# FFN buffers at the right end of SBUF, opened before the output projection; small token block last; layer norms by half blocks; the last f's products reordered

## The chip, the core and the metric

The kernel runs on one core of a Trainium2 chip. The metric is device time of one execution in microseconds (us), as the median of several runs. The engines are named as in the profile: PE (TensorE; PEld its weight loads), DVE (VectorE), ACT (ScalarE), POOL (GpSimd) and SP (SyncE, which here issues the DMAs, all in one queue). The order of the instructions on each engine is fixed when the kernel is built; while it runs, each engine works through its own row and waits at an instruction until what it needs is there.

## The reference

One decoder layer on 2048 prompt tokens, 16 meta tokens and 32 sample tokens, in fp32: two token mixers (retention and gated delta net), an output projection, and a dense FFN, each followed by a residual and a layer norm. The change touches the last part:

```python
def layer_norm(x, g, b):
    mu = jnp.mean(x, -1, keepdims=True)
    var = jnp.mean(jnp.square(x - mu), -1, keepdims=True)
    return (x - mu) * lax.rsqrt(var + LN_EPS) * g + b

def swiglu(h, w_gate_up, w_down):          # 1024 -> 2 x 2816 -> 1024
    gu = h @ w_gate_up
    return (jax.nn.silu(gu[..., :D_FF]) * gu[..., D_FF:]) @ w_down

hp = layer_norm(ALPHA * hp + mixed, ln1_g, ln1_b)
hp = layer_norm(ALPHA * hp + swiglu(hp, w_gate_up, w_down), ln2_g, ln2_b)   # and so for the samples hs
```

The outputs are the layer's result for the 2048 prompt tokens and the 32 sample tokens, and the new mixer states.

## The kernel before

`attention()` computes the input projection and both mixers (0 to about 1350 us) and leaves the mixed activations in DRAM (`mixd`). `project()` and `ffn()` follow.

Precision: every fp32 operand of a product is split into a high and a low fp32r part (`split`, L309 the copy, mostly on ACT, and L316 the difference on DVE or POOL), and `mm3` (L366) sums three matmuls, high x high, high x low, low x high.

`project()` walks over 17 tiles of tokens: 16 of 128 prompt tokens and one of the 32 sample tokens, in the order of the FFN's blocks. For tile i it runs 48 matmuls into two PSUM banks (tile `d`), evicts them with the residual (DVE, L1175), makes the layer norm, and writes `yd` (L1177) for the FFN's residual. Two tiles later it transposes the tile (PE, `tr`, L1185; ACT copies it to `xr`, L1186). When both tiles of a pair are transposed, POOL makes four sums `T` (L1198), and seven DMAs (L1205) write the pair's parts and sums to DRAM, to `bd`. A tile's inputs are fetched one tile ahead (`mr<-mixd`, `oy<-xhat`).

`ffn()` treats the tokens in three blocks. A block takes its tokens as pairs, so that a product of a 2 x 2 split of gate and up weights with a 2 x 2 split of the activations is made with seven block products instead of eight; n is the column count of such a product. Block 0 is the small one (four prompt tiles and the sample tile, n = 272), blocks 1 and 2 have six prompt tiles each (n = 384). For each block the seven token operands (b11, t2, t1, b21, t3, t4, b22) come back from `bd` through the ring `fr` (L1370) and are split (`tokens`). Then f runs from 0 to 21, over slices of 128 of the 2816 hidden columns. For f, `weights(f)` fetches 1 MB through `fr` (L1250), POOL makes four sums `S` (L1264), and a11, a12, a22 and the sums s12, s34 are split on ACT and DVE; this happens while f - 1 is computed. `gateup` runs the seven products X, Y, Z, X2, Y2, W, Z2 (12 matmuls each), and DVE and ACT combine them (`x1`, `u2`, `u3`, `z5`) and make silu(gate) x up as `fh`, `fl`. The down products of two f, one unit per half tile of tokens (six matmuls into a PSUM bank `d`, then an addition to `y` by DVE, L1356, for the first two f L1354), are spread over the next f by `step`: one unit per step, at most twelve per pair of f. Behind the last unit of a tile stands its layer norm and the DMA of its output (L1359): bn_stats (L284), bn_aggr (L287), rsqrt by bit shift and three Newton steps on a single column (L261 to L268, ten instructions on DVE), `lnnm` (L297), ACT for scale and bias (L300), DVE for the gain (L302), POOL for the offset (L304). Only the very last tile takes the short form on DVE alone (L291, L293). A block's last down units and layer norms therefore run during the next block's f = 0 and 1, together with that block's token splits. In the last block the last two f are handled one at a time (three units per step in f = 21), and what is left is run at the end.

All of FFN's SBUF pools are opened in `ffn()`, after the projection's were closed. Where they lie on memory that the projection or the attention used, their first writers wait until the last readers of that memory are done.

## Time and profile before

| | |
|---|---|
| median of 3 runs | 3085.02 us (3084.47 to 3089.49) |
| the profiled execution | 3085.82 us, span 3084.0 us |
| mean granted PE clock | 0.972 |
| busy in the span | PE 2889.0, DVE 2189.5, ACT 1139.4, POOL 1055.6 us |

Times in a trace count from the start of its span. The span ends with the last recorded instruction or transfer; the execution's own time is 1.82 us longer. A row of a group gives the line, engine, operation, `out<-in`, shapes and count, then busy us and mean ns, then the engine's idle time just before and what ended it. A busy PE need not be at full rate: the granted clock of a stretch (1.00 is full) stands beside it in the windows. One instruction's duration includes what it waits for inside the engine.

### The profile page before, as it was taken

To read this page: it belongs to the slowest core of one execution; us is meant where nothing else is said; L and a number is where in the kernel's file an instruction comes from. 1 tells how busy PE (TensorE), PEld (TensorE's weight loads), DVE (VectorE), ACT (ScalarE), POOL (GpSimd) and SP (SyncE) were. 2 spreads that over 40 slices of the span, in tenths; PEclk is the share of its full clock that TensorE was granted. 3 is DMA by queue.
4 is the path that set the end of the run, shared out by engine and by line. 5 is a ranking of instruction groups with operands and counts; after the bars stand their busy time and mean duration, and the time that the engine had idled before them with its cause. 6 is when DMAs were issued, how large, how long until landed. Compare 5 with 4: busy or idle time off the path is not lost.

```text
span 3084.0 us, 47091 instructions
## 1 busy us (share of the span) xinstructions
PE 2889.0 (94%) x17930; PEld 2564.3 (83%) x17930; DVE 2189.5 (71%) x4547; ACT 1139.4 (37%) x2571; POOL 1055.6 (34%) x927
## 2 busy tenths in 40 slices
PE   6999998999999999999959999989999999999995
PEld 6888887888888877887848888889999988999994
DVE  7778676666676676567767777896666689666667
ACT  2444433444443433432233333433333343333331
POOL 1332222221222122225644545354334335333332
PEclk8999998999999999999979999989999999999998
DMA  7544533443344323346652222432212243221211
GB/s 268 211 158 175 178 141 132 155 156 145 130 153 169 116 91 122 117 151 208 206 175 97 95 85 89 144 122 76 75 55 76 73 130 130 75 76 55 76 62 41
DMA packets 132275, 384.75 MB, mean 125 GB/s; under 512 B 18145, under 2 KB 53521, under 8 KB 115665
## 3 DMA queue, kind: packets, MB, share of 16 engines
q1 hardware_dynamic: 132048, 381.74, 35.5%
q8 instruction: 141, 2.31, 0.3%
q14 instruction: 86, 0.70, 0.1%
HBM read 294.14 MB, written 87.56 MB: 124 GB/s over the span
## 4 chain that ended last, share of the span: by engine, by line
PE 58%; DVE 22%; POOL 7%; issue 7%; ACT 4%; DMA 3%; SPq 0%; POOLq 0%; ACTq 0%; DVEq 0%
PE pj L366 17%; PE d L366 15%; POOL S L1264 4%; PE Y L366 4%; PE X L366 4%; PE Z L366 4%; PE W L366 2%; DVE dl L316 2%; DVE s34l L316 1%; ACT s34h L309 1%; DVE rqt L267 1%; POOL Lm L920 1%; DVE cacc L820 1%; DVE y L1356 1%; DVE lnst L284 1%
## 5 line engine op out<-in xcount | busy, mean ns | idle before, releaser
L366 PE MATMUL pj<-wh,xT 128*128 128x256 f32 (+2 forms) x2176 | 453.4, 296 | 9.1 <-ACT wh L309 3.7
L366 PE MATMUL pj<-xT,wh 128*128 128x512 f32 (+1 forms) x1280 | 378.2, 379 | 0.8 <-DVE kp L775 0.6
L366 PEld LDWEIGHTS pj<-wh,xT 128*128 128x128 f32 (+1 forms) x2176 | 354.4, 191 | 14.1 <-ACT wh L309 4.0
L366 PE MATMUL pj<-wl,xT 128*128 128x256 f32 (+3 forms) x1088 | 315.3, 290 | 0.5 <-POOL wl L316 0.5
L366 PE MATMUL d<-dl,fh 128*128 128x512 f32 (+1 forms) x748 | 299.9, 401 | 8.4 <-DVE dl L316 7.8
L366 PE MATMUL d<-dh,fh 128*128 128x512 f32 (+1 forms) x748 | 293.8, 393 | 6.6 <-DVE y L1356 6.5
L366 PE MATMUL d<-dh,fl 128*128 128x512 f32 (+1 forms) x748 | 297.2, 397 | 0.7 <-POOL fl L316 0.7
L316 POOL TENSOR_TENSOR fl<-ta,fh 128x384 fp32r<-128x384 f32 (+1 forms) x66 | 70.8, 1073 | 642.5 <-ACT fh L309 642.5
L1264 POOL TENSOR_TENSOR S<-fr 128x512 f32<-128x512 f32 x132 | 209.7, 1606 | 168.1 <-DVE s34l L316 108.6
L1356 DVE TENSOR_TENSOR y<-y,d 128x512 f32<-128x512 f32 (+1 forms) x352 | 238.9, 680 | 31.7 <-PE d L366 31.6
L366 PE MATMUL pj<-xT,wl 128*128 128x512 f32 (+1 forms) x640 | 228.9, 358 | 0.0
L366 PEld LDWEIGHTS pj<-xT,wh 128*128 128x128 f32 x1280 | 207.4, 191 | 19.6 <-DVE S L674 3.0
L366 PEld LDWEIGHTS pj<-wl,xT 128*128 128x128 f32 (+1 forms) x1088 | 207.6, 191 | 1.1 <-POOL wl L316 0.8
L366 PEld LDWEIGHTS d<-dl,fh 128*128 128x128 f32 (+1 forms) x748 | 137.9, 184 | 39.9 <-DVE dl L316 21.8
L366 PEld LDWEIGHTS d<-dh,fl 128*128 128x128 f32 (+1 forms) x748 | 137.9, 184 | 33.9 <-POOL fl L316 1.1
L316 DVE TENSOR_TENSOR a11l<-fr,a11h 128x512 fp32r<-128x512 f32 x66 | 52.1, 789 | 160.2 <-ACT a11h L309 160.2
L366 PEld LDWEIGHTS d<-dh,fh 128*128 128x128 f32 (+1 forms) x748 | 138.1, 185 | 29.4 <-DVE y L1356 9.8
L920 POOL TENSOR_TENSOR Lm<-LT,lvl 128x512 f16<-128x512 f32 (+1 forms) x108 | 138.4, 1315 | 35.0 <-DVE LT L908 28.5
L309 ACT CAST a11h<-fr 128x512 fp32r<-128x512 f32 x66 | 41.0, 621 | 293.4 <-DMA fr<-gu 293.4
L366 PE MATMUL X<-b,a11h 128*128 128x384 f32 (+1 forms) x528 | 125.6, 322 | 19.2 <-ACT b L309 13.9
L531 POOL TENSOR_TENSOR qk<-qk,rotB 128x256 f32<-128x256 f32 (+1 forms) x68 | 51.3, 759 | 259.2 <-DVE rotB L530 202.0
L366 PE MATMUL Y<-t,s12h 128*128 128x384 f32 (+1 forms) x528 | 129.2, 330 | 7.0 <-ACT s12h L309 2.5
(333 smaller groups left out, 7904.3 us busy)
## 6 DMA issues: line engine op xcount, KB each, us to landing
fr<-gu SPq DMA_DIRECT2D x132, 512.0 KB, 3.9
wh<-parts SPq DMA_DIRECT2D x45, 1024.0 KB, 6.2
wl<-parts SPq DMA_DIRECT2D x45, 1024.0 KB, 6.8
fr<-dn SPq DMA_DIRECT2D x66, 512.0 KB, 3.9
parts<-wh SPq DMA_DIRECT2D x15, 1024.0 KB, 6.4
parts<-wl SPq DMA_DIRECT2D x15, 1024.0 KB, 7.5
raw<-wret SPq DMA_DIRECT2D x16, 512.0 KB, 7.0
raw<-wgd SPq DMA_DIRECT2D x16, 512.0 KB, 6.5
```

Source lines behind the costliest of these rows:

```text
L267: nc.vector.scalar_tensor_tensor(out=t, in0=y, scalar=a, in1=y, op0=ALU.mult, op1=ALU.mult)
L284: i = nc.vector.bn_stats(out=st[:, o], in_=x)
L309: i = nc.scalar.copy(out=h, in_=src)
L316: i = (nc.vector if el == "dve" else nc.gpsimd).tensor_tensor(out=l, in0=src, in1=h.bitcast(F32), op=ALU.subtract)
L366: self.nc.tensor.matmul(out, lhsT=a(k), rhs=b(k), start=first and k == 0 and i == 0, stop=last and k == kn - 1 and i == 2, skip_group_chec ...
L531: nc.gpsimd.tensor_tensor(out=o, in0=o, in1=B[:, :, ::-1, :], op=ALU.add)
L820: nc.vector.scalar_tensor_tensor(out=ac, in0=pre[:, i:i + N], scalar=w(i), in1=ac, op0=ALU.mult, op1=ALU.add)
L920: nc.gpsimd.tensor_tensor(out=Lm[:, x - 1], in0=LT, in1=lvl(x), op=ALU.mult)
L1264: op = lambda o, x, z, f: nc.gpsimd.tensor_tensor(out=o, in0=x, in1=z, op=f)
L1356: nc.vector.tensor_tensor(out=ys, in0=ys, in1=p, op=ALU.add)
```

## The change

Five edits:

1. The pools `f_r` (the ring `fr`), `f_a` (split weights), `f_s` (sums S) and a new one for the token operand b11 (`f_b1`) are opened between `attention()` and `project()`, at the right-hand end of SBUF (`side="right"`), and stay open to the end of the FFN. To make room, the projection's pool of transposed tiles `o_x` has three buffers, not four. Code and dependencies of `weights` and `tokens` stay; with the memory free, the scheduler can place them earlier.
2. The prompt tiles are assigned to blocks so that the first two have six tiles (n = 384) and the last one four tiles and the sample tile (n = 272). The order of tiles in the projection follows; the sample tile is its last.
3. `down` takes the tiles in two groups, the pairs' first tiles (the sample tile not among them) and the others. Behind a group's last unit `layer_norms` does the norms of the whole group: bn_stats and bn_aggr per tile, one rsqrt on two or three columns (three instructions and three Newton steps of three, on [128, T]), one `lnnm`, then per tile ACT, DVE and two POOL additions as before, and the outputs' DMAs behind them. In the last block every second tile of a group takes four half-row instructions on DVE instead.
4. In the last f of the last block the order of products is X, Y, X2, Y2, W, Z, and `s4 x b22` into a second X bank, so that `ta` (the first half of silu) is made earlier; there is no copy z5. The differences `fl` of that f go to DVE, not POOL.
5. The gain and offset rows g2, b2 are loaded in `ffn()` as before; in the order their loads move from the attention to the end of the projection.

```diff
-    Block([(_P(0), _P(1), 128), (_P(2), _P(3), 128), (0, NS // 2, NS // 2)]),
-    Block([(_P(i), _P(i + 1), 128) for i in (4, 6, 8)]),
-    Block([(_P(i), _P(i + 1), 128) for i in (10, 12, 14)]),
+    Block([(_P(i), _P(i + 1), 128) for i in (0, 2, 4)]),
+    Block([(_P(i), _P(i + 1), 128) for i in (6, 8, 10)]),
+    Block([(_P(12), _P(13), 128), (_P(14), _P(15), 128), (0, NS // 2, NS // 2)]),
...
+    def layer_norms(self, work, g, b, pool, end=False):
+        nc = self.nc
+        T = len(work)
+        mv = pool.tile([128, 3, 2], F32, tag="lnm", name="lnm")[:, :T]
+        if any(rows < 128 for _, rows in work):
+            nc.gpsimd.memset(mv, 1.0)
+        for i, (x, rows) in enumerate(work):
+            st = pool.tile([128, 2, 6], F32, tag="lnst", name="lnst")[:rows]
+            for o in range(2):
+                nc.vector.bn_stats(out=st[:, o], in_=x[:, 512 * o:512 * o + 512])
+            nc.vector.bn_aggr(out=mv[:rows, i], in_=st)
+        r = self.rsqrt(mv[:, :, 1], T, 128, pool, 1.0, LN_EPS)
+        nm = pool.tile([128, 3], F32, tag="lnnm", name="lnnm")[:, :T]
+        nc.vector.scalar_tensor_tensor(out=nm, in0=mv[:, :, 0], scalar=-1.0, in1=r, op0=ALU.mult, op1=ALU.mult)
+        for i, (x, rows) in enumerate(work):
+            if end and i % 2:
+                for o in (slice(0, 512), slice(512, 1024)):
+                    nc.vector.scalar_tensor_tensor(out=x[:, o], in0=x[:, o], scalar=mv[:rows, i, 0:1], in1=g[:rows, o], op0=ALU.subtract, op1=ALU.mult)
+                    nc.vector.scalar_tensor_tensor(out=x[:, o], in0=x[:, o], scalar=r[:rows, i:i + 1], in1=b[:rows, o], op0=ALU.mult, op1=ALU.add)
+                continue
+            nc.scalar.activation(out=x, in_=x, func=AF.Identity, scale=r[:rows, i:i + 1], bias=nm[:rows, i:i + 1])
+            nc.vector.tensor_tensor(out=x, in0=x, in1=g[:rows], op=ALU.mult)
+            for o in (slice(0, 512), slice(512, 1024)):
+                nc.gpsimd.tensor_tensor(out=x[:, o], in0=x[:, o], in1=b[:rows, o], op=ALU.add)
...
-            xp = self.pool("o_x", bufs=4, es=s)
+            xp = self.pool("o_x", bufs=3, es=s)
...
-            ap = self.pool("f_a", es=s)
-            rp = self.pool("f_r", bufs=4, es=s)
-            sp = self.pool("f_s", es=s)
+            ap, rp, sp = self.fa, self.fr, self.fs
...
-                        self.split(t[:, c:c + m], fh[:, o:o + m], fl[:, o:o + m], "act", "pool")
+                        self.split(t[:, c:c + m], fh[:, o:o + m], fl[:, o:o + m], "act", "dve" if late else "pool")
...
+                if late:
+                    product(X, "a12", "b21", more=True)
+                    step(2)
+                    product(Y, "s3", "t3", more=True)
+                    add(u3, x1, Y)
+                    step(3)
+                    product(W, "a22", "t4")
+                    add(x1, u3, W)
+                    swish(X, x1, 0, "ta")
+                    step(4)
+                    product(Z, "s1", "t1")
+                    add(z5, u3, Z)
+                    add(u2, u2, Z)
+                    step(5)
+                    X = ps("X")
+                    product(X, "s4", "b22")
+                    add(u2, u2, X)
+                    swish(u2, z5, 1, "tb")
+                    step(6)
+                    return fh, fl
...
-                        if n and last:
-                            self.layer_norm(y[i][:rows], rows, g2, b2, sm, last == "end" and i == order[-1])
-                            nc.sync.dma_start(out=self.O["y"][r0:r0 + rows, :], in_=y[i][:rows])
+                            if last and n and i == group[-1]:
+                                self.layer_norms([(y[j][:tiles[j][1]], tiles[j][1]) for j in group], g2, b2, sm, last == "end")
+                                for j in group:
+                                    nc.sync.dma_start(out=self.O["y"][tiles[j][0]:sum(tiles[j]), :], in_=y[j][:tiles[j][1]])
...
-                for name in ORDER:
-                    t = bp.tile([128, 2, 4 * 384], F32R, tag=name, name=name)
+                for j, name in enumerate(ORDER):
+                    t = (self.fb if name == "b11" else bp).tile([128, 2, 4 * 384], F32R, tag=name, name=name)
...
-            with self.weights_es:
-                self.attention()
-                self.project()
-            self.ffn()
+            with ExitStack() as late:
+                with self.weights_es:
+                    self.attention()
+                    self.fr = self.pool("f_r", bufs=4, es=late, side="right")
+                    self.fa = self.pool("f_a", es=late, side="right")
+                    self.fs = self.pool("f_s", es=late, side="right")
+                    self.fb = self.pool("f_b1", es=late, side="right")
+                    self.project()
+                self.ffn()
```

What this does to the order is shown at two places. The first is SP's row, the one queue of DMAs. Before, around the end of the projection: `bd` are the last tile's parts and sums, `fr<-gu` the FFN's first weights, `fr<-bd` the first block's token operands.

```order
L1205 DMA bd<-xr 128x512 x2
L1177 DMA yd<-oy 128x1024
L1205 DMA bd<-T 128x512
L1205 DMA bd<-xr 128x512
L1205 DMA bd<-T 128x512 x3
L1250 DMA fr<-gu 128x1024 x2
L1370 DMA fr<-bd 128x544 x14
L1250 DMA fr<-gu 128x1024 x4
```

All FFN loads stand behind the last tile's parts. After, at the start of the projection, whose gain and offset rows are the first two lines:

```order
L379 DMA g_16830<-vec 128x1024
L379 DMA b_16832<-vec 128x1024
L1187 DMA mr<-mixd 128x8x128
L1276 DMA fr<-gu 128x1024 x2
L1205 DMA yd<-oy 128x1024
L1187 DMA mr<-mixd 128x8x128
L1205 DMA yd<-oy 128x1024
L1189 DMA oy<-xhat 128x1024
```

The first `fr<-gu` has moved ahead of the first tile's `yd`. And after, from the last of the sample tile's parts to the weights of the next two f (`vec` are g2 and b2, `y_19010` the residual of the first block):

```order
L1233 DMA bd<-xr 512x1x16
L379 DMA g_18630<-vec 128x1024
L379 DMA b_18632<-vec 128x1024
L1419 DMA fr<-bd 128x512
L1419 DMA fr<-bd 128x1024
L1419 DMA fr<-bd 128x512
L1419 DMA fr<-bd 128x1024
L1419 DMA fr<-bd 128x512
L1454 DMA y_19010<-yd 128x1024
L1276 DMA fr<-gu 128x1024 x4
```

Nine of the first block's fourteen `fr<-bd` stand within the projection, ahead of the rows shown last; g2, b2, the five remaining `fr<-bd` and a first residual tile now stand between the last `bd` and the next weights.

The second is DVE's row in f = 1 of the second block, where the first block's layer norms are made. Before (`rqt`, `rqy` are the Newton steps of one tile, `a11l`, `a12l` the weight splits, `z`, `u` the sums of products):

```order
L267 SCALAR_TENSOR_TENSOR rqt<-rqy,rqa 128x1
L1301 TENSOR_TENSOR z_22888<-u_22887,z_22888 128x384
L268 SCALAR_TENSOR_TENSOR rqy<-rqt,rqy 128x1
L284 BN_STATS lnst<-y_19015 128x6
L316 TENSOR_TENSOR a11l<-fr,a11h 128x512
L267 SCALAR_TENSOR_TENSOR rqt<-rqy,rqa 128x1
L1301 TENSOR_TENSOR u_22887<-u_22887,W 128x384
L268 SCALAR_TENSOR_TENSOR rqy<-rqt,rqy 128x1
L284 BN_STATS lnst<-y_19015 128x6
L267 SCALAR_TENSOR_TENSOR rqt<-rqy,rqa 128x1
L316 TENSOR_TENSOR a12l<-fr,a12h 128x512
L268 SCALAR_TENSOR_TENSOR rqy<-rqt,rqy 128x1
```

After (`rqa`, `rqt`, `rqy` hold three tiles in three columns):

```order
L263 TENSOR_SCALAR rqa<-lnm 128x3
L1404 TENSOR_TENSOR y_19012<-y_19012,d 128x512
L264 TENSOR_SCALAR rqt<-rqa 128x3
L344 TENSOR_TENSOR s12l<-S,s12h 128x1024
L265 TENSOR_SCALAR rqy<-rqt 128x3
L1404 TENSOR_TENSOR y_19012<-y_19012,d 128x512
L273 TENSOR_TENSOR rqt<-rqy 128x3
L318 BN_STATS lnst<-y_19012 128x6
L274 SCALAR_TENSOR_TENSOR rqt<-rqt,rqa 128x3
L318 BN_STATS lnst<-y_19012 128x6
L275 SCALAR_TENSOR_TENSOR rqy<-rqt,rqy 128x3
L344 TENSOR_TENSOR a12l<-fr,a12h 128x512
```

Before, such a chain of six Newton instructions stands in the row for each of the tiles; after, one chain of nine stands for three tiles, among the same other work, and it starts when the third tile's bn_aggr is done.

39 lines of the change are left out of this document (21 added, 18 removed).

## The prediction

> **What bounds the kernel now.** The page first: its span and TensorE's row.
>
> ```profile
> span 3084.0 us, 47091 instructions
> ...
> PE 2889.0 (94%) x17930; PEld 2564.3 (83%) x17930; DVE 2189.5 (71%) x4547; ACT 1139.4 (37%) x2571; POOL 1055.6 (34%) x927
> ```
>
> PE is busy for 94%, so 195 us of the span are idle; what can be won is idle time or time at a low clock. The table of windows around the end of the output projection comes next (stretch, length, then busy us and instruction count of PE, PEld, DVE, ACT, POOL, then granted clock, DMA share, GB/s).
>
> ```profile
> 1362.00:1550.00 188.00, 187.52 (x882) 152.12 (x883) 133.47 (x274) 48.66 (x61) 106.06 (x75) 1.00 0.62 195
> 1550.00:1560.00 10.00, 2.09 (x17) 1.65 (x15) 7.85 (x15) 3.30 (x5) 5.01 (x5) 0.79 0.53 198
> 1560.00:1570.00 10.00, 2.23 (x8) 1.43 (x8) 0.00 (x0) 1.17 (x2) 7.41 (x6) 0.50 0.48 184
> 1570.00:1585.00 15.00, 3.25 (x10) 2.48 (x11) 9.60 (x9) 6.71 (x10) 6.13 (x4) 0.50 0.50 163
> 1585.00:1640.00 55.00, 46.49 (x281) 42.06 (x280) 47.23 (x59) 25.59 (x47) 26.91 (x19) 0.89 0.49 161
> ```
>
> The projection itself is PE-bound: 187.52 of 188. Behind it, from 1550 to 1640, PE works 2.09 + 2.23 + 3.25 + 46.49 = 54 us of 90 and at a clock of 0.50 to 0.89. The timelines say why (start, duration, engine, line, operation): DVE's rows of the last tile's layer norm, a POOL row beside them, PE's rows and the DMA queue's (there the duration is that of issuing), and one row of the waits (us in all, times, longest).
>
> ```profile
> 1550.25 0.69 DVE L1175 SCALAR_TENSOR_TENSOR oy<-oy,d 128x512 f32<-128x512 f32 x1 [3.28 <-PE d L366]
> ...
> 1555.15 1.30 DVE L267 SCALAR_TENSOR_TENSOR rqt<-rqy,rqa 128x1 f32<-128x1 f32 x1
> ...
> 1556.69 0.22 DVE L267 SCALAR_TENSOR_TENSOR rqt<-rqy,rqa 128x1 f32<-128x1 f32 x1
> ```
>
> ```profile
> 1553.84 2.60 POOL L1198 TENSOR_TENSOR T<-xr,T 128x512 f32<-128x512 f32 x2
> ```
>
> ```profile
> 1561.28 2.34 PE L1185 MATMUL tr<-ident,oy 128*128 128x128 f32 x8 [9.19 <-POOL oy L304]
> ...
> 1584.49 0.59 PE L366 MATMUL X<-b,a11h 128*128 128x272 f32 x1 [0.72 <-DVE b L316]
> ```
>
> ```profile
> 1566.87 1.66 SPq L1205 DMA_DIRECT2D bd<-T  x3
> 1570.29 0.81 SPq L1250 DMA_DIRECT2D fr<-gu  x2
> 1571.15 23.29 SPq L1370 DMA_DIRECT2D fr<-bd  x14
> 1594.92 4.11 SPq L1250 DMA_DIRECT2D fr<-gu  x4
> ```
>
> ```profile
> POOL S L1264 <- DMA fr<-gu: 6.5, 1, 6.5
> ```
>
> The last eviction starts at 1550.25 (call it t0), that tile is transposed at 1561.28, and its sums and their DMAs follow until 1568.5. Only then does SP issue the first FFN weights (1570.29) and 14 token loads one behind the other for 23.29 us. PE starts the FFN in earnest at 1584.49, t0 + 34.2; f = 1's weights are not asked for before 1594.92, t0 + 44.7.
>
> The second place is the change of token block. Four windows: the first 136 us of block 1, a steady stretch with 384 columns, the first 138 us of block 2, a steady one with 272 columns.
>
> ```profile
> 1974.40:2110.00 135.60, 123.88 (x603) 110.65 (x602) 120.11 (x198) 55.02 (x83) 62.20 (x44) 0.94 0.41 139
> 2200.00:2246.00 46.00, 45.74 (x240) 42.24 (x239) 30.30 (x43) 15.05 (x24) 17.16 (x12) 1.00 0.21 69
> 2501.80:2640.00 138.20, 125.09 (x612) 113.38 (x611) 125.35 (x212) 55.84 (x83) 65.98 (x44) 0.95 0.42 143
> 1700.00:1736.00 36.00, 35.94 (x233) 32.12 (x232) 27.09 (x40) 14.03 (x27) 17.89 (x16) 1.00 0.27 93
> ```
>
> Steady, PE does 240 matmuls in 46.0 us (192 ns each) with DVE at 30.30. At that rate the 603 and 612 matmuls of the transitions are worth 115.6 and 117.3 us; they took 135.6 and 138.2, so each transition loses about 20 us, with DVE 89 to 91% busy. DVE is the limit there. Its groups and POOL's largest that come with the old block's layer norm, in the second transition:
>
> ```profile
> L267 DVE SCALAR_TENSOR_TENSOR rqt<-rqy,rqa 128x1 f32<-128x1 f32 x18 | 10.5, 586 | 0.0
> L268 DVE SCALAR_TENSOR_TENSOR rqy<-rqt,rqy 128x1 f32<-128x1 f32 x18 | 10.2, 568 | 0.0
> ```
>
> ```profile
> L304 POOL TENSOR_TENSOR y<-y,b 128x512 f32<-128x512 f32 x12 | 17.1, 1443 | 21.7 <-DVE y L302 15.8 <-DVE rqa L265 5.9
> ```
>
> The 36 Newton instructions on one column take 20.7 us, 575 ns each on average, and up to 1.30 us under a POOL instruction (1555.15 above) where the same one takes 0.22 without (1556.69).
>
> The third is the tail, from the end of the last gate-up product at 3040.2: windows, DVE's groups, POOL's last rows.
>
> ```profile
> 3040.20:3060.00 19.80, 10.57 (x39) 6.26 (x38) 19.63 (x59) 3.53 (x4) 3.78 (x4) 0.94 0.07 26
> 3060.00:3084.00 24.00, 0.00 (x0) 0.00 (x0) 17.96 (x50) 3.72 (x3) 10.09 (x8) 0.50 0.27 110
> ```
>
> ```profile
> L1356 DVE TENSOR_TENSOR y<-y,d 128x512 f32<-128x512 f32 x13 | 8.7, 672 | 0.1
> L284 DVE BATCH_NORM_STATS2 lnst<-y 128x6 f32<-128x512 f32 x12 | 8.0, 673 | 0.0
> L267 DVE SCALAR_TENSOR_TENSOR rqt<-rqy,rqa 128x1 f32<-128x1 f32 x18 | 7.7, 442 | 0.0
> L302 DVE TENSOR_TENSOR y<-y,g 128x1024 f32<-128x1024 f32 x5 | 6.1, 1213 | 0.0
> L268 DVE SCALAR_TENSOR_TENSOR rqy<-rqt,rqy 128x1 f32<-128x1 f32 x18 | 4.7, 266 | 0.1
> ```
>
> ```profile
> 3077.51 2.92 POOL L304 TENSOR_TENSOR y<-y,b 128x512 f32<-128x512 f32 x2 [3.11 <-DVE y L302]
> ```
>
> DVE is busy 19.63 + 17.96 = 37.6 of 43.8 us and PE has nothing after 3060: evictions and layer norms on DVE end the kernel, then POOL's last two adds (to 3080.43) and the output's DMA.
>
> **The change part by part.** *Early FFN buffers.* By the new order the loads of weights(0) stand early in the projection, those of b11, t2 and t1 within it, and so do their splits and sums. Added there: four POOL sums,
>
> ```profile
> L1264 POOL TENSOR_TENSOR S<-fr 128x512 f32<-128x512 f32 x132 | 209.7, 1606 | 168.1 <-DVE s34l L316 108.6
> ```
>
> 4 x 1.6 = 6.4 us, and the splits of one f and of three token sums on ACT and DVE (in a steady stretch all that DVE does for two f is 27 to 30 us). In the projection's window POOL is idle for 82 us, DVE for 55, ACT for 139, so they hide. What may not hide is SP: a token load waits until the sums that it reads have landed, and the next tile's loads stand behind it.
>
> ```profile
> bd<-xr SPq DMA_DIRECT2D x24, 256.0 KB, 4.8
> ```
>
> A tile comes every 11.9 us (56 PE instructions of the window's 882 in 188 us) and its loads are issued one tile ahead, so a wait of 4.8 us fits; three o_x buffers in place of four hold the pair that is summed and the next tile. I charge 1 us (0 to 5).
>
> At the end of the projection PE still stands in order behind the last tile's transposes: t0 + 11.0 + 2.34 = t0 + 13.4. X follows it, but t2's and t1's splits now lie between that layer norm's instructions on ACT and DVE and push it back; I take t0 + 17.5 (13.4 to 24). Gain 34.2 - 17.5 = 16.7. Behind that, x1's pool opens only when the projection's are released, after the last small sums have been written (a bd issue takes 1.66/3 = 0.55 us, seven of them 3.9), and f = 1's weights are queued behind five token loads of 23.29/14 = 1.66 us, g2, b2 and a y tile: at about t0 + 38 in place of t0 + 44.7. On the other side the first block now has 384 columns: (46.0/240 - 36.0/233 = 0.038 us) x some 114 matmuls = 4.3 us more of its own work per f, 13 us in three f, under the same loads. I take 8 of these 13 and give back 3 for the wait on the pools: +5 (-3 to +13). Together 22 us (14 to 30).
>
> *Layer norms by half blocks.* Per 384-column block the small instructions of rsqrt fall from 6 x 11 = 66 to 2 x 13 = 26, the Newton ones among them from 36 to 18. At 0.575 us these give back 10.4 us, the other 22 at 0.15 to 0.22 another 3.3 to 4.8: 14 us of DVE. It can't give back more than the 20 us lost. The adds on POOL are the same 12, but six come in a row (6 x 1.44 = 8.6 us) and the sums of f + 2 and the splits `fl` wait behind them; the new y tiles can be fetched only after three outputs have left. From 384 to 384 columns I take 9 of the 14. From 384 to 272, DVE's slack in a steady stretch is 36 - 27.09 = 8.9 us instead of 15.7, so more of the old layer norm stays exposed: 5. Together 14 (5 to 22).
>
> The Trainium skill, "SBUF — State Buffer", section "Who interferes with whom", says that a DVE instruction with two SBUF inputs and a GpSimd instruction that reads SBUF exclude each other for whole instructions. The trace agrees: 1.30 us against 0.22. By that rule each of the 18 Newton instructions left could stand behind a whole POOL add of 1.44 us, 26 us in all, and six adds in a row make that likelier; the transitions would then give nothing, and the sum 3058.
>
> *Small block last, last tile's products reordered.* The block sizes are the same, so PE's sum stays. In the tail the last f has 10 evictions, 10 bn_stats and two grouped rsqrt in place of 13, 12 and six. In rows: -3 x 0.67 - 2 x 0.67 = -3.4; the 36 Newton instructions (7.7 + 4.7 = 12.4) become 18 at 0.27, -7.5; some 20 other small ones fewer, -3; two multiplies fewer, -2.4; four more half-row instructions at 0.75, +3; one more add, and `fl` on DVE instead of POOL, +1.2. That is -12 in rows, which overlap a little; I take -10, so DVE's 37.6 becomes 27.6. Behind the last product PE has 30 matmuls left instead of the 39 of the window's row, so it comes 9 x 188/882 = 2 us later, and the last POOL queue is four adds instead of two (1.46 each, one hidden), +1.4. Net 10 - 2 - 1.4 = 6.6; I take 6 (2 to 11).
>
> Sum against the profiled execution: 3085.82 (span 3084.0) - 22 - 14 - 6 + 1 = 3044.8. That execution lies 0.8 above the median of 3085.02, so the forecast is **3044**.
>
> **The rivals.** *A: the start isn't won.* X is early, but the other products of f = 0 and all of f = 1 stand behind the pools' release, g2, b2 and the token loads in SP's one queue, and PE waits there for what it waited for before X. For it: 23.29 us of serial token issues and the wait of 6.5 us of S on f's weights. Against it: nine of the loads are done before. Start 6 instead of 22: 3060.
>
> *B: the transitions get nothing, or worse.* Six adds in a row on POOL and three outputs in a row on SP hold back S and with it s12, s34; DVE is relieved but isn't what ends the wait. For it: POOL already spends 17.1 us there and the block with 272 columns has little slack. Against it: DVE is 91% busy. Transitions -5 instead of 14: 3063. The rule of the skill above ends here too.
>
> *A and B together*: gains 6 - 5 + 6 - 1 = 6, within the noise: 3079.
>
> *C, slower: SP holds the projection.* Token loads and weights in the projection wait at the head of the one queue, and mr/oy of the next tile come late; with o_x at three the transposes wait as well. PE was 99.7% busy there, so each us shows. With gains of 42 elsewhere the sign turns at 42/16 = 2.6 us per tile, and from 3.0 it is slower by more than the noise; at 3.2 us (two thirds of 4.8) 16 tiles cost 51: 3094. Against it: only nine such loads are there, each with a tile's time of slack.
>
> *D: the change doesn't do what it says*, the early pools having to wait for attention's memory: the order shows their loads ahead of the first projected tile's output, so this comes out as A.
>
> **How the numbers follow.** Forecast 0.66, A with D 0.15, B 0.13, both 0.03, C 0.03. The terms' bounds (8, 9, 5, 4 us either way, taken as independent) give about 13; A and B reach to 3063. Low: 3044 - 22, where start, transitions and tail all lie near their upper ends; high 3064. So 3022 to 3064. About 0.2%, 6 us, can be told from no change: faster 0.94, same 0.03, slower 0.03.
>
> **What would show it.** Right: the first X product 15 to 19 us behind the last eviction of the projection, f = 1's weights issued about 38 behind it; projection tiles still 11.8 us apart; PE busy at least 93% in the first 135 us of the second block, with 18 Newton instructions there; from the last gate-up product to the end about 36 us instead of 43.9. Wrong: projection tiles over 12.5 us apart (C), PE idle behind x1 or S for more than 15 us after its first X (A), POOL's adds as the releaser of S in the transitions (B).

## The result and the profile after

The changed kernel takes 3070.22 us (median of 4 runs, 3063.84 to 3072.64) against 3084.74 for the kernel before in the same runs: a ratio of 0.9946, 95% interval 0.9928 to 0.9964. It is faster by 14.5 us. 41 were forecast, and the time lies 6 us above the range.

The page of the changed kernel; its profiled execution took 3072.64 us:

```profile
span 3070.9 us, 46987 instructions
...
PE 2892.9 (94%) x17930; PEld 2567.4 (84%) x17930; DVE 2172.0 (71%) x4444; ACT 1135.8 (37%) x2569; POOL 1059.5 (35%) x923
```

To see where the gain is lost, both traces were cut into the same stages at the rows of ACT's copy of X to `x1`, one per f. The work of a stage is counted in matmuls, at the spacings of undisturbed stretches. A projection tile (a row of the chain of work) gives a down or projection matmul:

```profile
1389.55 10.90 PE d L394 x48
```

That is 10.90/48 = 0.227 us. A steady pair of f has 168 gate-up matmuls and 72 (384 columns) or 60 (272) down matmuls; with 46.37 and 35.29 us in the kernel before, a gate-up matmul takes 0.1786 or 0.1289 us. What a stage takes beyond its matmuls is called its loss. The start runs from the last eviction of the projection to the x copy of f = 5; a block change runs from the x copy of the old block's f = 21 to that of the new block's f = 6 (work 154.6 us for 272 to 384 columns, 163.7 for 384 to 384, 132.6 for 384 to 272).

| us | before | changed | gain | forecast |
|---|---|---|---|---|
| loss at the start | 49.8 | 29.6 | 20.2 | 22 |
| projection, first to last eviction | 195.0 | 194.0 | 1.0 | -1 |
| loss at the first change | 19.9 (272 to 384) | 15.8 (384 to 384) | | |
| loss at the second change | 20.1 (384 to 384) | 30.9 (384 to 272) | both: -6.7 | 14 |
| a steady pair, 384 columns | 46.37 | 46.52 | -2.2 in all | 0 |
| last x copy to the end | 73.9 | 59.4, with 9.0 less work | 5.4 | 6 |
| first projection eviction to the end | 1728.8 | 1710.9 | 17.9 | 41 |

The -2.2 are 15.5 steady pairs outside the other stages, at 0.145 us each. The gains by stage add up to 17.7. In the attention before them only the loads of g2 and b2 were moved, and still the first projection eviction came 4.7 us later in this execution. Over the twenty kernels profiled here it came between 1352.0 and 1362.3 us, whatever had been changed, and its time goes with the granted clock of the first 600 us: 0.97 in the six earliest executions (1352.0 to 1355.2), 0.95 in the five latest (1359.9 to 1362.3, the changed kernel's among them). That scatter is why the losses by stage say more below than the medians do.

The start after the change, in windows (columns as in the prediction), and two DMA rows:

```profile
1360.00:1553.90 193.90, 193.34 (x909) 156.35 (x908) 150.08 (x290) 55.96 (x72) 116.13 (x79) 1.00 0.63 207
1553.90:1563.90 10.00, 1.95 (x17) 1.50 (x14) 9.71 (x17) 4.97 (x8) 7.32 (x5) 0.83 0.57 184
1563.90:1575.00 11.10, 5.59 (x24) 5.32 (x25) 4.59 (x6) 4.28 (x6) 6.00 (x7) 0.54 0.63 186
1575.00:1640.00 65.00, 56.84 (x295) 52.45 (x294) 47.74 (x56) 26.13 (x42) 29.99 (x20) 0.97 0.57 193
```

```profile
1577.75 7.26 SPq L1419 DMA_DIRECT2D fr<-bd  x5
...
1586.97 5.52 SPq L1276 DMA_DIRECT2D fr<-gu  x4
```

The last eviction starts at 1553.95. PE's first X matmul starts at 1570.67, 16.7 us behind it (17.5 forecast), and f = 1's weights are asked for 33 us behind it (38 forecast); from 1575 on PE is busy for 56.84 of 65 us at a clock of 0.97, where it had 46.49 of 55 at 0.89.

The second block change as one window, and what POOL does in it (start, duration, operation, count, and in brackets its idle time before and the releaser):

```profile
2583.30:2746.80 163.50, 143.97 (x825) 125.63 (x824) 128.25 (x207) 64.83 (x111) 77.20 (x59) 0.94 0.37 120
```

```profile
2653.15 4.43 POOL L332 TENSOR_TENSOR y<-y,b 128x512 f32<-128x512 f32 x2 [10.69 <-DVE y L330]
2657.54 0.77 POOL L344 TENSOR_TENSOR fl<-ta,fh 128x272 fp32r<-128x272 f32 x1
2658.28 6.41 POOL L332 TENSOR_TENSOR y<-y,b 128x512 f32<-128x512 f32 x4
2664.65 2.95 POOL L344 TENSOR_TENSOR fl<-tb,fh 128x256 fp32r<-128x256 f32 x2
2667.55 3.04 POOL L1290 TENSOR_TENSOR S<-fr 128x512 f32<-128x512 f32 x2
...
2680.83 5.56 POOL L332 TENSOR_TENSOR y<-y,b 128x512 f32<-128x512 f32 x2 [7.61 <-DVE y L330]
2686.36 0.96 POOL L344 TENSOR_TENSOR fl<-ta,fh 128x272 fp32r<-128x272 f32 x1
2687.27 5.60 POOL L332 TENSOR_TENSOR y<-y,b 128x512 f32<-128x512 f32 x4
2692.84 2.52 POOL L1290 TENSOR_TENSOR S<-fr 128x512 f32<-128x512 f32 x2
```

```profile
ACT s12h L337 <- POOL S L1290: 19.8, 4, 9.0
POOL y L332 <- DVE y L330: 18.3, 2, 10.7
```

The waits are those of the stretch from 2620 to 2715 (us in all, times, longest). DVE is busy for 128.25 of 163.5 us, 78%. POOL stands idle for 10.69 and 7.61 us at the head of a group's additions until DVE has made the first multiply, works off six of them and one `fl` in 12 us, and only then come the sums S of the next weights, for which ACT (`s12h`) waits 19.8 us in all.

The first change as one window:

```profile
2056.10:2235.60 179.50, 168.47 (x848) 153.84 (x847) 148.41 (x212) 70.80 (x106) 79.99 (x55) 0.97 0.36 125
```

The tail, from the last x copy to the last gate-up product and from there to the end:

```profile
3011.50:3034.30 22.80, 22.80 (x132) 18.73 (x131) 15.86 (x27) 3.65 (x7) 0.97 (x3) 1.00 0.00 1
3034.30:3070.90 36.60, 7.92 (x33) 4.80 (x31) 27.58 (x67) 4.55 (x6) 8.82 (x6) 0.70 0.16 61
```

DVE does 27.58 us of work behind the last product, as forecast (27.6).

### The profile page after: what moved, and what is told of

Its sections match the earlier page's. It is cut to its first block, busy times and chain, and to the rows that moved or that the text cites. A ratio compares the mean times of both kernels' runs of the same rounds, so it can differ in the third digit from the quotient of the medians.

```text
span 3070.9 us, 46987 instructions
## 1 busy us (share of the span) xinstructions
PE 2892.9 (94%) x17930; PEld 2567.4 (84%) x17930; DVE 2172.0 (71%) x4444; ACT 1135.8 (37%) x2569; POOL 1059.5 (35%) x923
## 4 chain that ended last, share of the span: by engine, by line
PE 67%; DVE 20%; ACT 3%; issue 3%; POOL 3%; DMA 2%; SPq 0%; ACTq 0%; POOLq 0%; DVEq 0%
PE d L394 19%; PE pj L394 17%; PE Y L394 5%; PE X L394 5%; PE Z L394 5%; PE W L394 4%; DVE dl L344 3%; DVE s34l L344 1%; DMA fr<-bd 1%; ACT s34h L337 1%; DVE cacc L848 1%; POOL S L1290 1%; POOL y L332 1%; PE w L965 1%; DVE tb L1335 1%
## 5 line engine op out<-in xcount | busy, mean ns | idle before, releaser
L394 PE MATMUL d<-dl,fh 128*128 128x512 f32 (+1 forms) x748 | 299.5, 400 | 14.7 <-DVE dl L344 11.6
L394 PE MATMUL d<-dh,fh 128*128 128x512 f32 (+1 forms) x748 | 300.1, 402 | 9.7 <-DVE y L1402 6.2
L394 PEld LDWEIGHTS d<-dl,fh 128*128 128x128 f32 (+1 forms) x748 | 138.7, 185 | 46.7 <-DVE dl L344 28.3
L394 PEld LDWEIGHTS d<-dh,fh 128*128 128x128 f32 (+1 forms) x748 | 138.4, 185 | 30.5 <-DVE y L1402 6.6
L394 PEld LDWEIGHTS pj<-xT,wl 128*128 128x128 f32 x640 | 121.4, 190 | 15.8
L394 PE MATMUL Y<-t,s34h 128*128 128x384 f32 (+1 forms) x528 | 126.7, 325 | 6.5 <-ACT t L337 3.1
```

Of the source, the lines that this page charges most:

```text
L394: self.nc.tensor.matmul(out, lhsT=a(k), rhs=b(k), start=first and k == 0 and i == 0, stop=last and k == kn - 1 and i == 2, skip_group_chec ...
```

## The experiments

Each run's median is given with that of the kernel before on the same chip. Losses are those of the start, the first and the second change, in us. Kernels with the same instructions at the changes (the changed one, e5 and e21; and e10, e16, e17, e19 and e20) differ by up to 3 us in one of the two losses there and by up to 2 us in their sum; smaller differences between two runs count for nothing.

### Undoing and isolating the parts

`e1_ln_by_tile` makes the norms at the block changes tile by tile again:

```diff
-                            if last and n and i == group[-1]:
+                            if n and last == "block":
+                                self.layer_norm(y[i][:rows], rows, g2, b2, sm)
+                                nc.sync.dma_start(out=self.O["y"][r0:r0 + rows, :], in_=y[i][:rows])
+                            elif last and n and i == group[-1]:
```

> The changed kernel with one thing undone: at the two block changes the layer norms are made tile by tile again, as before the change (the tail keeps its grouped norms). Losses over the steady pace, from the rows of the changed kernel: 15.8 us at its first block change, 31.0 at its second. Theory P (the six grouped offset adds stand ahead of the sums S in POOL's row, and POOL sits idle in front of them until DVE has multiplied; S and the next weights come late): both losses fall to about the 20 us of the kernel before or less, 6 to 12 us faster than the changed kernel, 3058 to 3064, and POOL no longer waits over 7 us for a multiply with S behind. Theory B (the order of the blocks: 272 columns leave too little room on DVE for the norms of six tiles): no change, 3070, or some us slower since 40 small DVE instructions per change come back. Theory Q (three outputs in a row hold the weight loads in SP's queue): as P, but the weights' loads, not POOL, are the releaser of S.

Measured: 3074.4 against 3086.2; losses 30.4, 20.4, 32.6. Grouping is worth 4.6 us at 384 to 384 and 1.7, within the scatter, at 384 to 272; it is not what makes the second change dear. As I had put it, theory P should have gained here, and it did not; what this run leaves in place is the twelve additions on POOL.

`e2_small_first` puts back the old `BLOCKS`.

> The changed kernel with the small block first again (272, 384, 384 columns); everything else stays, the tail too, which then has six tiles. Theory B (the change from 384 to 272 columns is what costs): the 31.0 us at the second change become about 16 as at the first; at the start the early buffers hide less under 272 columns (4 us less per f), the tail has two evictions and two norms more (+3): 3058 to 3064. Theory P: a grouped norm costs whatever the block's width, so only the width of the following block matters little: 3066 to 3074.

Measured: 3071.07 against 3086.2; losses 38.7, 21.1 (272 to 384), 15.0 (384 to 384). In the medians the block order is no gain or loss that can be told: it wins 9 us at the start and 5 in the tail and gives 11 back at the changes (36.1 lost with the small block first, 46.7 with it last). The tail of this run, with six tiles, the new products and the grouped norms, takes 73.6 us from the last x copy; before it took 73.9. The part behind its last gate-up product:

```profile
3029.00:3073.00 44.00, 12.16 (x42) 8.29 (x40) 34.51 (x73) 5.78 (x6) 12.11 (x8) 0.62 0.18 72
```

DVE has 34.51 us of work there for the 37.6 before, and the stretch is as long as before: what the grouped norms spare isn't on the path.

`e3_pools_alone` is the kernel before with the early pools and three o_x buffers alone.

> The kernel before with the early FFN pools alone (and three o_x buffers): blocks, norms and tail as before. The start gained 20 us against the last eviction of the projection in the changed kernel, of which the width of the first block should be a part (4 us of cover per f): 12 to 20 us faster than before here, 3065 to 3073. If the start were won by the width alone: under 8 us, above 3077. If the early pools slow the attention or the projection (there the changed kernel's trace is 4.7 us late before the first tile), the first eviction of the projection is again 4 to 5 us late; if that lateness is a matter of the run, it is not.

Measured: 3079.14 against 3086.2 (0.9975, 0.9964 to 0.9987); losses 38.3, 19.7, 18.8, and the steady pair is 46.52. The start wins 11.5 us here; 8.7 more come in the changed kernel, and 9.1 of them go when its small block is put first again (38.7 above): with the pools early, that is the width of the first block.

`e4_groups_alone` is the kernel before with grouped norms at the block changes alone.

> The kernel before with the grouped layer norms at the two block changes alone (tail by tile, blocks 272, 384, 384). Theory P: 40 small DVE instructions fewer at each change, but POOL's six adds hold S: between 4 us faster and 8 us slower than 3084.7. My prediction's step (DVE is the limit, 7 us won per change): 3070. Theory B: both changes lead into 384 columns, so each gains what the first change of the changed kernel gained, 4 us: 3077.

Measured: 3083.78 against 3086.2 (0.9990, 0.9981 to 0.9998); losses 49.1, 20.8, 14.0. Grouping wins 6 us at 384 to 384 and nothing at 272 to 384, though the durations of DVE's instructions add up to 6 to 8 us less at both; DVE's busy time falls by 3.8 us (143.68 to 139.93) and 4.8 us (151.85 to 147.05). The small instructions give back more than that, and others take it. Rows of a change from 384 to 384 columns, in the kernel before (2479.8 to 2663.5) and in the changed kernel (2056.1 to 2235.6):

```profile
L302 DVE TENSOR_TENSOR y<-y,g 128x1024 f32<-128x1024 f32 x6 | 7.3, 1221 | 1.3 <-ACT y L300 1.2
```

```profile
L330 DVE TENSOR_TENSOR y<-y,g 128x1024 f32<-128x1024 f32 x6 | 9.2, 1583 | 0.0
...
L275 DVE SCALAR_TENSOR_TENSOR rqy<-rqt,rqy 128x3 f32<-128x3 f32 x6 | 2.0, 329 | 0.1
L273 DVE TENSOR_TENSOR rqt<-rqy 128x3 f32<-128x3 f32 x6 | 1.9, 314 | 0.1
L274 DVE SCALAR_TENSOR_TENSOR rqt<-rqt,rqa 128x3 f32<-128x3 f32 x6 | 1.9, 312 | 0.0
```

The Newton instructions take 5.8 us where they took 20.7, but each multiply takes 1583 ns for 1221.

`e5_old_products` is the changed kernel with `late` never true, so that the last f has its old order.

> The changed kernel with the last f's products in the order of before (and the differences fl of that f on POOL); the small block stays last and the tail's norms stay grouped. In the changed kernel the tail from the last x copy to the end is 59.4 us. If the reordered products are worth what I charged to them with the small block (some 2 to 3 us of the 6 in the tail): 3072 to 3074, tail 61 to 63. If the small block alone makes the tail shorter (the run with six tiles in the tail and the new products had the tail of before): 3070, tail 59 to 60.

Measured: 3071.08 against 3085.86; the tail from the last x copy is 59.6 us (59.4 in the changed kernel). With the tail of `e2_small_first` this says that reordered products and grouped norms are worth 0.2 to 0.3 us there; the small block alone makes the tail shorter. At the two changes, where its instructions are those of the changed kernel, this run loses 17.8 and 29.6.

### What sets the block change

`e6_no_adds` leaves out the offset additions at the block changes, `e7_no_norms` the whole norms there:

```diff
-            for o in (slice(0, 512), slice(512, 1024)):
+            for o in () if not end else (slice(0, 512), slice(512, 1024)):
                 nc.gpsimd.tensor_tensor(out=x[:, o], in0=x[:, o], in1=b[:rows, o], op=ALU.add)
...
-                                self.layer_norms([(y[j][:tiles[j][1]], tiles[j][1]) for j in group], g2, b2, sm, last == "end")
+                                if last == "end":
+                                    self.layer_norms([(y[j][:tiles[j][1]], tiles[j][1]) for j in group], g2, b2, sm, True)
```

> The changed kernel without the offset additions of the norms at the two block changes (the outputs of those twelve tiles lack the offset), so that POOL's row holds no adds there. Losses of the changed kernel: 15.8 us (384 to 384) and 31.0 (384 to 272). Theory P (POOL's row holds S behind the six adds): the second falls by 10 or more, the first by 5 or more. Theory D (DVE's own work at a block change is the limit: 142 us of it lie in the 163.5 us of the second change, for 132.6 of PE): the adds only lengthen DVE's instructions where they collide, so 0 to 6 us at each change.

> The changed kernel without any layer norm at the two block changes (the outputs of those twelve tiles are left as they are before the norm); token loads, outputs and their waits on the residual additions stay. Theory D: 25 us of DVE work go per change; the loss from 384 to 272 falls from 31 to 5 to 12, the one from 384 to 384 from 15.8 to under 6. If the token loads and their ring of four buffers in SP's queue are the limit: over 20 stays at the second change. Theory P: also under 12, but then the run without the adds does nearly the same.

Measured: 3042.56 and 3042.59 against 3085.86; losses 30.5, 9.2, 16.0 without the additions and 30.4, 9.3, 10.5 without any norm. Both changes as windows, without the additions and then without norms:

```profile
2052.90:2225.80 172.90, 166.26 (x849) 151.80 (x848) 138.88 (x212) 70.70 (x106) 60.16 (x43) 0.99 0.39 130
2573.40:2722.00 148.60, 136.97 (x832) 121.58 (x831) 124.50 (x207) 65.19 (x110) 58.87 (x47) 0.99 0.40 132
```

```profile
2055.80:2228.80 173.00, 167.65 (x848) 153.24 (x847) 120.31 (x162) 64.56 (x100) 59.41 (x43) 0.98 0.39 130
2576.30:2719.40 143.10, 136.75 (x826) 121.94 (x825) 106.26 (x157) 58.07 (x105) 56.41 (x47) 0.98 0.41 138
```

At 384 to 384 the additions are all that the norms cost PE: taking away another 19 us of DVE's time (138.88 and 120.31) changes nothing (9.2 and 9.3). At 384 to 272 they are 14.9 of 20.4. That alone doesn't settle theory D, since taking the additions away also shortens DVE's other instructions: at the first change the same 212 are busy for 148.41 us with the additions and 138.88 without, at the second the same 207 for 128.25 and 124.50. Of the 14.9 us, 7 are PE's own busy time at a lower granted clock (143.97 us for 825 recorded matmuls at 0.94, 136.97 for 832 at 0.99).

`e9_dve_norms` uses the half-row form on DVE for all norms at the block changes (`if not end or i % 2:`), `e10_dve_adds` moves the offset additions to DVE as one whole row, `e11_half_adds` the second half-row only:

```diff
-            for o in (slice(0, 512), slice(512, 1024)):
-                nc.gpsimd.tensor_tensor(out=x[:, o], in0=x[:, o], in1=b[:rows, o], op=ALU.add)
+            if end:
+                for o in (slice(0, 512), slice(512, 1024)):
+                    nc.gpsimd.tensor_tensor(out=x[:, o], in0=x[:, o], in1=b[:rows, o], op=ALU.add)
+            else:
+                nc.vector.tensor_tensor(out=x, in0=x, in1=b[:rows], op=ALU.add)
```

> The changed kernel with all norms at the block changes in the form of two half-row instructions twice on DVE: no ACT, no POOL adds, DVE has 6 x (4 x 0.75 - 1.2) = 11 us more per change. Theory D: losses 8 to 12 us larger at each change, about 24 and 41. Theory P: smaller by 5 to 10 at each.

> The changed kernel with the norms' offset additions at the two block changes moved from POOL to DVE, one whole-row addition per tile (7 us more of DVE per change, POOL's row as in the run without adds). Losses so far, 384 to 384 and 384 to 272: changed kernel 15.8 and 30.9, without adds 9.2 and 16.0, without norms 9.3 and 10.5, all norms on DVE 14.7 and 23.0. Theory P (POOL's row, not DVE's sum, sets the block change): 9 to 14 and 16 to 22, 3048 to 3056 us, faster than the form with all norms on DVE. Theory D (DVE's sum is the limit): as with all norms on DVE or worse, 14 and 23, 3058.

> As the run with the additions on DVE, but of each row only the second half; the first half stays on POOL (six adds per change there instead of twelve, still behind DVE's multiply). If the waiting place in POOL's row is what costs (an add stands ahead of S until the multiply is done), one add per tile waits as long as two: losses near the changed kernel's 15.8 and 30.9, less 4 to 8 together. If it is the 17 us of adding that costs: half way between the changed kernel and the run with all additions on DVE.

Measured: 3058.53 against 3085.86 for all norms on DVE (losses 29.9, 14.7, 23.0). There theory D wanted 8 to 12 us more at each change and theory P 5 to 10 less; it was 1.1 and 7.9 less. Then 3053.42 against 3086.58 for the additions on DVE (0.9902, 0.9888 to 0.9917; losses 28.9, 12.2, 21.6); 3055.92 against 3086.58 for half of them (30.1, 13.5, 24.8). With twelve, six and no additions on POOL the two losses are 15.8 and 30.9, 13.5 and 24.8, 12.2 and 21.6, although DVE takes over what POOL gives up. POOL's rows in the second change, additions on DVE:

```profile
2651.32 4.55 POOL L1293 TENSOR_TENSOR S<-fr 128x512 f32<-128x512 f32 x2 [1.81 <-DVE s34l L347]
...
2675.07 3.09 POOL L1293 TENSOR_TENSOR S<-fr 128x512 f32<-128x512 f32 x2 [2.65 <-DVE s34l L347]
```

The sums of the same f start at 2651.32 there, 79.9 us behind the stage's first x copy (2571.47), and at 2667.55 in the changed kernel, 84.3 behind 2583.28; those of the next f at 2675.07 (103.6) and 2692.84 (109.6). Some of the additions' cost also lies inside DVE's own instructions. Three of DVE's groups in that window, changed kernel and additions on DVE:

```profile
L344 DVE TENSOR_TENSOR dl<-fr,dh 128x1024 fp32r<-128x1024 f32 x7 | 10.5, 1512 | 0.1
L344 DVE TENSOR_TENSOR s34l<-S,s34h 128x1024 fp32r<-128x1024 f32 x7 | 10.3, 1476 | 0.6 <-ACT s34h L337 0.5
...
L330 DVE TENSOR_TENSOR y<-y,g 128x1024 f32<-128x1024 f32 x6 | 8.1, 1396 | 0.0
```

```profile
L347 DVE TENSOR_TENSOR s34l<-S,s34h 128x1024 fp32r<-128x1024 f32 x7 | 8.5, 1213 | 0.5 <-ACT s34h L340 0.5
L347 DVE TENSOR_TENSOR dl<-fr,dh 128x1024 fp32r<-128x1024 f32 x7 | 8.3, 1205 | 0.0
...
L330 DVE TENSOR_TENSOR y<-y,g 128x1024 f32<-128x1024 f32 x6 | 7.1, 1216 | 0.0
```

The same instructions take 1512, 1476 and 1396 ns on average over the change with POOL's additions and 1205, 1213 and 1216 without. That is the exclusion of DVE's two-input instructions and GpSimd's that the Trainium skill states ("SBUF — State Buffer", section "Who interferes with whom"); these rows agree with it.

How much of the loss is this and how much POOL's row can be read from DVE's busy time in the window of each change, set beside the loss (us):

| run | additions on POOL per change | 384 to 384: DVE busy, loss | 384 to 272: DVE busy, loss |
|---|---|---|---|
| `e7_no_norms` | none | 120.3, 9.3 | 106.3, 10.5 |
| `e6_no_adds` | none | 138.9, 9.2 | 124.5, 16.0 |
| `e10_dve_adds` | none | 143.6, 12.2 | 128.2, 21.6 |
| `e9_dve_norms` | none | 146.5, 14.7 | 131.3, 23.0 |
| `e11_half_adds` | six | 146.9, 13.5 | 133.5, 24.8 |
| `e4_groups_alone` | twelve | 147.1, 14.0 | |
| changed | twelve | 148.4, 15.8 | 128.3, 30.9 |
| `e12_before_dve_adds` | none | 151.7, 18.0 | |
| before | twelve | 151.9, 20.1 | |
| `e1_ln_by_tile` | twelve | 152.9, 20.4 | 136.6, 32.6 |

From 384 to 384 columns the loss follows DVE's busy time within the scatter, whoever makes the additions, down to some 139 us; there 9 us are left that no edit here takes away. So theory D holds for this change, and POOL's additions cost there by lengthening DVE's instructions.

From 384 to 272 they cost more than that. At 127.7 to 128.5 us of DVE, as in the changed kernel, the five runs that have its grouped norms with all additions on DVE (e10, e16, e17, e19 and e20) lose 21.6 to 22.7 us for its 30.9: 8 to 9 us are POOL's row. Without additions on POOL the loss goes with DVE's time here too (10.5, 16.0, 21.6 and 23.0). The wait for the multiply in POOL's row seems not to be what makes the 8 to 9 us: with half the additions POOL still stands idle for 10.53 and 8.36 us in front of them, and the loss is little above that of `e9_dve_norms`. That would leave the time that the additions take ahead of S, which is not shown; a run that moved them behind S without removing them was not made. Theory Q isn't what these edits win back: three outputs in a row stand in SP's queue in the changed kernel and in `e10_dve_adds`, and at the second change S waits once for `fr<-gu` in both, 12.5 us in the changed kernel and 11.8 with the additions on DVE.

`e12_before_dve_adds` makes that edit in the kernel before, `e13_dve_adds_small_first` is `e10_dve_adds` with the old `BLOCKS`.

> The kernel before with that one edit (offset additions of the norms at the block changes on DVE, whole rows; everything else as before). Its losses are 19.9 (272 to 384) and 20.1 (384 to 384). Theory P holds for tile-by-tile norms too: 12 to 16 each, 3074 to 3079 us. Theory D: DVE, 91% busy there, gets 7 us more: 24 to 28 each, 3090 to 3098.

> The run with the additions on DVE, with the small block first. It tells what the block order is worth when POOL no longer sets the change: start 9 us worse (38.5 instead of 29.7 lost), tail 8 us worse, the two changes 272 to 384 and 384 to 384 at 12 to 15 and 9 to 14 instead of 9 to 14 and 16 to 22. So 8 to 14 us slower than that run, 3058 to 3068. If the last block's 272 columns cost more than that at the change, they come out the same.

Measured: 3083.63 against 3086.58 for the first (0.9997, 0.9988 to 1.0006: no change that can be told), losses 49.4, 16.4, 18.0, so 5.6 us less at the changes. In groups, and with the small block first in both, moving them wins 6.7 (36.1 in `e2_small_first`, 29.4 in `e13_dve_adds_small_first`), which can't be told from 5.6: it is the small block at the end, not the grouping, that makes POOL's additions dear (12.9, from 46.7 to 33.8). The second: 3065.01 against 3086.58, losses 36.7, 16.7, 12.7. It is 11.6 us slower than `e10_dve_adds`, as expected: without the additions on POOL, putting the small block last costs 4.4 us at the changes (29.4 and 33.8) in place of 10.6, and its gains at the start and in the tail are left.

### What wins the start

`e16_splits_left` and `e17_b11_left` are `e10_dve_adds` with one pool each opened in `ffn()` among the others again (`f_a`, or b11's). `e18_before_right` is the kernel before with three pools only moved to the right end:

```diff
-            ap = self.pool("f_a", es=s)
-            rp = self.pool("f_r", bufs=4, es=s)
-            sp = self.pool("f_s", es=s)
+            ap = self.pool("f_a", es=s, side="right")
+            rp = self.pool("f_r", bufs=4, es=s, side="right")
+            sp = self.pool("f_s", es=s, side="right")
```

> The run with the additions on DVE, with the pool of split weights f_a opened with the FFN's other pools again (not early, not at the right end); the ring, S and b11 stay early. It asks for the two terms of the early pools apart: the start (loss 28.9 to 30.5 us with all four) and the steady pair of f at 384 columns (46.51 us with them, 46.37 without). If f_a's place is what lengthens the pair: 46.37 again, 3 us back over two blocks; if not, 46.51. At the start a11's and s12's splits then wait for the projection's memory: X later by 4 to 10 us, so 3054 to 3062 in all.

> The same question for b11's pool: opened with the FFN's other pools, while ring, S and f_a stay early at the right end. If b11's place or its own pool lengthens the pair: 46.37; if not, 46.51. At the start X then waits for b11's load and split, 3 to 8 us later; 3054 to 3061 in all.

> The kernel before with its ring, f_a and S at the right end of SBUF but opened in the FFN as before: only their addresses change, not when they open. If the address is what lengthens the steady pair: 46.52 instead of 46.37 in the second and third block and 3 us slower than before, 3087 to 3090. If opening them early is: 46.37 and no change. The start should stay at its loss of 50 us unless the place alone frees the memory earlier.

Measured: 3053.57, 3057.67 and 3073.18, each against 3088.73. The start loses 29.1 with f_a put back and 30.0 with b11 put back, against 28.9 with all four early: neither is needed early, though X had been expected to come 3 to 10 us later in both. In the kernel before, the place alone takes the start's loss from 49.8 to 34.1, 4 us better than the early pools did (38.3); its ratio is 0.9957 (0.9943 to 0.9971), nearly that of the whole change. Expected was no gain, unless the place alone freed the memory earlier. Its first weights are issued at 1370.31, 181 us ahead of the last eviction, where before they came 20 us behind it. Its first X product:

```profile
1568.01 0.82 PE L368 MATMUL X<-b,a11h 128*128 128x272 f32 x2 [0.68 <-ACT xr L1188]
```

`e21_change_right_in_ffn` is the changed kernel with ring, f_a and S at the right end but opened in `ffn()`, b11 among the others and four o_x buffers; `e19_right_in_ffn` is the same with the additions on DVE, and `e20_ring_right` also takes f_a back to the left.

> The changed kernel with one part undone: the pools stay at the right end but are opened in the FFN (b11 among the others, four o_x buffers). If opening them early is what won the start: loss 40 or more instead of 29.6, 3080. If the place is: 24 to 32, 3066 to 3072.

> The run with the additions on DVE, with ring, f_a and S at the right end of SBUF but opened only with the FFN's other pools, b11 among the others, and four o_x buffers again. In the kernel before, that place alone took the loss at the start from 49.8 to 34.1 us, more than the early pools did there (38.3). If the place is what frees the loads, not the time of opening: start loss 24 to 30 (28.9 with the early pools), 3048 to 3054 us. If the first block of 384 columns needs b11 early: loss 32 to 38, 3056 to 3062.

> The same with f_a among the FFN's other pools (left) and only the ring and S at the right end. Steady pairs at 384 columns 46.40 us instead of 46.50 (as when f_a alone was put back), 2 us over two blocks; the start within 3 us of the run with f_a at the right. 3046 to 3053 us.

Measured: 3072.37, 3057.27 and 3055.08, each against 3085.92; start losses 29.4, 30.8 and 33.4. In the changed kernel the early opening is worth 0.2 us (29.6 with it, 29.4 without): the start is won by the place and the first block's width, which is worth 4.7 us there (34.1 and 29.4). The start of `e19_right_in_ffn` lies just above its range for that case (24 to 30), the median of `e20_ring_right` 2 us above its own. The steady pair shows whose place costs: two x copies of one odd and one even f, 46.37 us apart before, 46.51 in the changed kernel, 46.40 with f_a back at the left (`e16_splits_left`):

```profile
2201.54 0.48 ACT L1315 COPY x<-X 128x384 f32<-128x384 f32 x1 [2.10 <-PE X L366]
...
2247.91 0.48 ACT L1315 COPY x<-X 128x384 f32<-128x384 f32 x1 [2.10 <-PE X L366]
```

```profile
2211.17 0.48 ACT L1341 COPY x<-X 128x384 f32<-128x384 f32 x1 [2.13 <-PE X L394]
...
2257.68 0.48 ACT L1341 COPY x<-X 128x384 f32<-128x384 f32 x1 [2.13 <-PE X L394]
```

```profile
2203.78 0.48 ACT L1345 COPY x<-X 128x384 f32<-128x384 f32 x1 [2.13 <-PE X L397]
...
2250.18 0.48 ACT L1345 COPY x<-X 128x384 f32<-128x384 f32 x1 [2.13 <-PE X L397]
```

It is 46.36 in `e20_ring_right`, 46.49 in `e18_before_right` and 46.50 with b11 put back. So f_a's address makes the difference, of about 0.6 ns per matmul (with f_a at the left, pools opened behind it in `ffn()` move too, which no run separates); why is not known.

The best of these kernels is the changed one with the additions on DVE: 3053.42 (3048.73 to 3057.57), 33 us under the kernel before on the same chip, more than twice the change's gain; with f_a back at the left it is the same within the scatter (0.9888, 0.9872 to 0.9905).

## Why the prediction was wrong

The start came out in size: 20.2 us for 22, X at t0 + 16.7 for 17.5. The mechanism was only half right. I credited the opening ahead of the projection; the place at the right end alone does it. The reason I see is that a pool on memory that nobody else uses has nothing to wait for, wherever it is opened in the program; the weights' early issue in `e18_before_right` fits it, but no run shows who used that memory. The share of the wider first block, which I took as 8 less 3 us, was 8.7 to 9.1 with the pools early and 4.7 with the place alone.

The projection came out at a gain of 1 where I charged 1: neither the three o_x buffers nor the token loads in SP's queue delayed it (rival C).

The tail came out at 5.4 for 6, but by the small block alone, so that the size was luck. That grouped norms and reordered products help there was wrong: 0.2 to 0.3 us with six tiles and with five.

The step that failed is the one on the block changes: "From 384 to 384 columns I take 9 of the 14. From 384 to 272 [...] 5. Together 14". Measured were 4.3 and, against the kernel before's 19.9 at 272 to 384, -11.0.

Its first term, 14 us of DVE given back by the small instructions of a change, was much too large. They did give it back (the Newton instructions fell from 20.7 to 5.8 us), but beside POOL's additions the whole-tile instructions grew, and DVE's busy time at 384 to 384 fell by 3.4 us only (151.85 to 148.41). I had taken an instruction's time, waits inside it included, as time that goes with the instruction. That DVE is the limit there was right: the loss follows its busy time, and fell by 4.3. The rival by which each of the 18 Newton instructions left stands behind a whole addition, 26 us in all, didn't come either; it was the multiplies and splits that were held up. So grouping, for which the sum has 18 us (9 at each change), is worth 4 to 6 at both together: the losses add up to 40.0 before and 34.8 in `e4_groups_alone`, to 34.4 in `e12_before_dve_adds` and 29.4 in `e13_dve_adds_small_first`, to 53.0 in `e1_ln_by_tile` and 46.7 in the changed kernel.

Its second term, 4 us for the narrower block, was 10.6 (36.1 in `e2_small_first`, 46.7 in the changed kernel). With the additions off POOL it is 4.4: the price in DVE's slack was about right, and what got no price of its own is POOL's row, worth 8 to 9 us at 384 to 272. That is rival B, for the second change only. I had named it with its place and priced it at -5 for both changes (measured -6.7, near by luck, since the first change gained), but gave it 0.16 and held against it that DVE is 91% busy. POOL's share of 34% of the span doesn't show it either: its row is in fixed order, and products that others wait for stand behind the additions. Behind a wide block the narrow one also has 31 us less of PE work (132.6 for 163.7) under nearly the same norms and weights: even without any norm it loses 10.5.

With B's case, 3063, and the steady pair's 2.2 us that I had not seen (the address of f_a), the sum is 3065; the rest is within the runs' scatter. The range ended at 3064, since I counted A and B as its far end and left no room for a term that no row of before shows.

## What to carry to other kernels

Before crediting a stall to the busiest engine, take the work of a lightly loaded one beside it away in an experiment: here moving twelve additions per block change from the engine busy for a third to the one that looked full won 33 us in place of 14. It did so with the small block last; in the kernel before the same move won nothing that can be told. And what a change takes from an engine is read from its busy time, not from the instructions that go: where two engines hold each other up, other instructions can take the time. Where a buffer's place lets its stage's loads start early, opening its pool early adds nothing: here it was 0.2 us. And if a reordering moves a narrower stage behind a wide one, ask what the wide stage leaves to be done, for the narrow one has less work to hide it under.

## What was not expected of the hardware

A pair of f with its 168 gate-up matmuls of 384 columns and 72 down matmuls took 46.35 to 46.40 us with the split weights in one part of SBUF and 46.49 to 46.52 in another. With 272 columns there was no such difference between the kernel before and the changed one (35.30 and 35.28); in other kernels the last block's pair took 35.0 to 35.2 with the weights in either part (35.08 in `e16_splits_left`, 35.12 in `e10_dve_adds`), for a reason that wasn't looked for. And the same kernel's executions differ by up to 18 us: those of `e3_pools_alone` took from 3070.33 us, at a mean granted clock of 0.978, to 3087.97, at 0.971.
